# A hybrid two-layer decoder on one core: the stick-breaking rounds in a written order, and the value projections regrouped

## The chip, the cores and the metric

The kernel runs on one core of one Trainium2 chip. The metric is the device time of one execution in microseconds (us), the median of several runs. Names of engines are those of the profile: PE (TensorE, matmuls), PEld (its weight loads), DVE (VectorE), ACT (ScalarE), POOL (GpSimd) and SP (SyncE, which issues DMAs).

## The reference

The reference is a trunk of two decoder layers over 512 positions of width 1024. Each layer has a mixer and a gated feed-forward part with a short causal convolution. The change touches only the mixer of the second layer (`odd_mixer`):

```
cq, ck, cv, sq, sk, sv = split_cols(h @ w_in, ODD_SPLITS)
o_dil = dilated_attention(groups(cq), groups(ck), groups(cv), slopes)
o_sb  = stick_breaking_attention(heads(sq), heads(sk), heads(sv))
return concat([o_dil, o_sb]) @ w_out
```

Dilated attention has three groups of four heads: a plain group (window 128, dilation 1) and two strided groups (dilations 4 and 16). The three are merged by their softmax denominators. Stick-breaking attention has four heads. For each head, with strictly causal entries only:

```
z = (q @ k.T) * scale
log_keep = log_sigmoid(-z)
after = reversed cumsum of log_keep over the keys, without the own key
a = exp(log_sigmoid(z) + after);   o = a @ v
```

## The kernel before, in words

**Numbers.** Every float32 product with weights is made of two rounded parts, a high and a low one (`wh`, `wl`; `xh`, `xl`), by `mm3` (L317 to L319): three matmuls, high by high, high by low, low by high. The class `Weights` loads each weight unit (128 x 1024) into a raw buffer by a DMA on SP's queue (L60), and splits it: ACT casts the high part (L82), DVE subtracts (L83). There are 3 raw buffers (`wraw`) and 5 pairs of split weights (`wh`, `wl`), both used in turn; a load waits until its raw buffer's last split is done, a split waits until the matmuls of the unit five places earlier are done. `W.ahead(n)` puts the splits of all units up to n into the program at that place; `W.depth` is how far ahead `next()` reaches.

**The order of the work.** Outside of `tc.manual_schedule` a scheduler of the compiler decides the order of each engine's instructions. Inside it, the engines that are named keep the order in which the Python code emits. Each engine then works strictly through its own list, and waits where an operand or a buffer isn't ready.

**The stage around the change** (function `odd`), in order:

1. The values of both strided groups (`av`, 512 columns, L1480 to L1495): four tiles of 128 positions, 24 matmuls of 512 columns each. ACT evicts each tile to `vst` (L1493) and issues four DMAs (L1495) which sort its rows by position mod 4 into `cv12`.
2. Four projections of 24 matmuls (`proj_T`, tile `apt`): `sq` and `sk`, each for two pairs of heads.
3. The stick-breaking values (`proj_V(sv)`, tile `apv`, L1458 to L1472): four tiles of 24 matmuls of 256 columns.
4. Two rounds `u` of stick-breaking, each with a pair of heads. Per round: 16 score matmuls (`zp`, L1523), DVE adds the mask (L1527) and takes the minimum with 40 (L1533), ACT takes exp (L1534) and then ln(1 + x) (L1539), DVE takes the maximum with `z` (L1540), and the result is split into `sh` (ACT, L225) and `sl` (DVE, L226). Then, for three blocks of keys from the last to the first, matmuls with a triangle of ones give the sums over later keys (`run` L1552, `cp` L1558), DVE adds them to `z` (L1560, L1562) and ACT takes exp (L1565). At the end 16 matmuls with the values (`osb`, L1571). Between these the code emits the strided groups' eight `proj_T` (list `T12`), four in each round; the scheduler mixes their matmuls with the rounds'. `sh` and `sl` have one buffer each, so the second head's split waits for the first head's sums.
5. Under a written order: four `proj_T` for the plain group, each followed by scores of the strided groups (`score12`, L1606, with exps on ACT, L1617); then the plain group's values (`proj_V(cv)`, again 256 columns), between whose tiles stand the plain group's scores (`score0`, L1631, exps L1640).
6. Still under that order: statistics are exchanged through DRAM (L1661, L1662), `share` turns them into factors, DVE scales (L1679, L1709), PE transposes (L1689, L1719), ACT evicts the transposed blocks to `pt` (L1690, L1720), and PE multiplies them with the values (L1668). `todo` lists eight such blocks, and block n is transposed while block n-1 is multiplied. Here stand also the splits of one output weight `wo` and of the next weight units (`W.ahead`).
7. The output projection (`ao`), then the second feed-forward part.

Of the kernel before, what the change touches and what calls it, by code (L numbers as in the profile page):

```python
# [9 lines left out]
F32 = mybir.dt.float32  # L10
# [7 lines left out]
P = 128  # L18
# [78 lines left out]
def trunk(tc, A, out):  # L97
# [3 lines left out]
    with ExitStack() as top:  # L101
# [1315 lines left out]
        def odd(xnT, pending, order):  # L1417
            xh, xl = xnT
            with ExitStack() as es:
# [4 lines left out]
                cv12 = ap.tile([P, 4, 512], F32, tag="cv12", name="cv12")  # L1424
# [8 lines left out]
                spare = [ap.tile([P, 4, 256], F32, tag=f"spare{n}", name="spare") for n in range(2)]  # L1433
# [4 lines left out]
                sv = sb.tile([P, NT, 256], F32, tag="sv", name="sv")  # L1438
# [4 lines left out]
                def proj_T(dst, scale, permuted, on_act):  # L1443
                    acc = bank("a", "apt")
                    wh, wl = W.next()
                    for k in range(KD):
                        mm3(acc[:], wh[:, k * P:(k + 1) * P], wl[:, k * P:(k + 1) * P],
                            xh[:, k], xl[:, k], k == 0, k == KD - 1)
                    src, d = acc[:], dst[:]
                    if permuted:  # L1450
                        src = src.rearrange("p (t r) -> p r t", r=4)
                        d = d.rearrange("p (r t) -> p r t", r=4)
                    if on_act:
                        ACT.activation(d, src, AF.Copy, scale=scale)
                    else:
                        DVE.tensor_scalar(d, src, scale, None, ALU.mult)

                def proj_V(dst):  # L1458
                    ws = [W.next() for _ in range(2)]

                    def tile_V(i):
                        t = slice(i * P, (i + 1) * P)
                        a = bank("a", "apv")
                        for k in range(KD):
                            wh, wl = ws[k // 4]
                            c = slice((k % 4) * 256, (k % 4 + 1) * 256)
                            mm3(a[:, :256], xh[:, k, t], xl[:, k, t], wh[:, c], wl[:, c], k == 0, k == KD - 1)
                        if i % 2:
                            DVE.tensor_copy(dst[:, i], a[:, :256])
                        else:  # L1470
                            ACT.copy(dst[:, i], a[:, :256])

                    return tile_V
# [3 lines left out]
                ws = [W.next() for _ in range(4)]  # L1477
                W.depth = 5
                for i in ORDER:
                    t = slice(i * P, (i + 1) * P)  # L1480
                    a = bank("a", "av12")
                    at, *parts = pending.pop(0) if pending else (KD, )
                    for k in range(KD):
                        if k == at:
                            for f in parts:
                                f()
                        wh, wl = ws[k // 2]
                        c = slice((k % 2) * 512, (k % 2 + 1) * 512)
                        mm3(a[:], xh[:, k, t], xl[:, k, t], wh[:, c], wl[:, c], k == 0, k == KD - 1)
# [3 lines left out]
                    ACT.copy(st[:], a[:])  # L1493
                    for r in range(4):
                        nc.scalar.dma_start(cv12[32 * i:32 * i + 32, r], st[r::4, :])  # L1495
# [6 lines left out]
                ACT.copy(lead[0:1, 1:2], st[0:1, 0:1])  # L1502
# [6 lines left out]
                tile_V = proj_V(sv)  # L1509
                for i in ORDER:  # L1510
                    tile_V(i)
# [3 lines left out]
                def sb_scores(u):  # L1515

                    zs = [sb.tile([P, 1280], F32, tag="z", name="z", bufs=2) for _ in range(2)]
                    for n, (j0, o0, o1) in enumerate(spans):
                        zp = [bank(t, "zp") for t in ("ss", "nt", "aa")[n]]
                        for j in (j0,) if j0 < 2 else (2, 3):  # L1520
                            for y in range(2):
                                r = slice(y * 64, y * 64 + 64)
                                PE.matmul(zp[y][:, off[j] - o0:off[j + 1] - o0], sk[u][r, j * P:(j + 1) * P],  # L1523
                                          sq[u][r, j * P:], start=True, stop=True)
                        for y in range(2):
                            for j in (j0,) if j0 < 2 else (2, 3):
                                DVE.tensor_tensor(zs[y][:, off[j]:off[j + 1]], zp[y][:, off[j] - o0:off[j + 1] - o0],  # L1527
                                                  smask[:, :S - j * P], ALU.add)

                    sps = []  # L1530
                    for z in zs:
                        sp = sb.tile([P, 1280], F32, tag="sp", name="sp", bufs=2)
                        DVE.tensor_scalar(sp[:], z[:], 40.0, None, ALU.min)  # L1533
                        ACT.activation(sp[:], sp[:], AF.Exp)  # L1534
                        sps.append(sp)
                    return list(zip(zs, sps))

                def sb_softplus(z, sp):
                    ACT.activation(sp[:], sp[:], AF.Ln, bias=1.0)  # L1539
                    DVE.tensor_tensor(sp[:], z[:], sp[:], ALU.max)  # L1540

                def sb_weights(z, sp):
                    sh = sb.tile([P, 1280], F32R, tag="sh", name="sh")
                    sl = sb.tile([P, 1280], F32R, tag="sl", name="sl")
                    split(sh[:], sl[:], sp[:])


                    run = bank("t", "run")
                    for j in reversed(range(NT - 1)):
                        c, n = off[j], S - j * P  # L1550
                        for part in (sh, sl):
                            PE.matmul(run[:, (j + 1) * P:], tri[:, 1], part[:, off[j + 1]:off[j + 2]],  # L1552
                                      start=(j == NT - 2 and part is sh), stop=(part is sl), skip_group_check=True)
                        zp = bank("ssn"[j], "cp")
                        for i in (3, 2) if j == 2 else (j, ):
                            o, w = 256 * (i == 3), S - i * P
                            for part in (sh, sl):
                                PE.matmul(zp[:, o:o + w], tri[:, 0], part[:, off[i]:off[i] + w],  # L1558
                                          start=(part is sh), stop=(part is sl))
                        DVE.tensor_tensor(z[:, c + P:c + n], z[:, c + P:c + n], run[:, (j + 1) * P:], ALU.add)  # L1560
                        w = n + (P if j == 2 else 0)
                        DVE.tensor_tensor(z[:, c:c + w], z[:, c:c + w], zp[:, :w], ALU.add)  # L1562
                        if j < 2:
                            e = slice(c, 1280 if j else off[1])
                            ACT.activation(z[:, e], z[:, e], AF.Exp)  # L1565

                def sb_values(u, a, o):
                    for j in reversed(range(NT)):
                        for n in range(2):
                            h = 2 * u + n  # L1570
                            PE.matmul(o[n * 64:(n + 1) * 64, j * P:], sv[:, j, h * 64:(h + 1) * 64],  # L1571
                                      a[n][:, off[j]:off[j + 1]], start=(j == NT - 1), stop=(j == 0),
                                      skip_group_check=True)

                T12 = [lambda t=t, x=x: proj_T(t[x], (-0.125, 1.0)[t is ck], True, t is cq)
                       for x in range(2, 6) for t in (cq, ck)]
                for u in range(2):
                    zs = sb_scores(u)
                    for _ in range(2):
                        T12.pop(0)()  # L1580
                    for v in zs:
                        sb_softplus(*v)
                    T12.pop(0)()
                    for v in zs:
                        sb_weights(*v)
                    T12.pop(0)()
                    o = bank("o", "osb")
                    sb_values(u, [z for z, _ in zs], o)
                    split(oS[0][:, u], oS[1][:, u], o)


                s12, s0 = {}, {}

# [78 lines left out]
                def turned_to(n):  # L1672
                    tag, pool = (("spare0", ap), ("spare1", ap), ("sl", sb))[n % 3]
                    return pool.tile([P, 4, 256], F32, tag=tag, name="pt")[:]
# [6 lines left out]
                def turn0(i):  # L1681
                    def f():
                        w = span0[i][1]
                        pt = turned_to(i)
# [26 lines left out]
                def turn12(hp, rp):  # L1711
                    def f():
                        s = s12[hp, rp]
                        pt = turned_to(2 * hp + rp).rearrange("p (y a) (b c) -> p y a b c", y=2, b=2)
# [21 lines left out]
                homes = [[(sb, "sq"), (sb, "sk")], [(sb, "sv"), (ap, "tab12")]]  # L1736
# [3 lines left out]
                with tc.manual_schedule(engines={PE.engine, DVE.engine, ACT.engine, POOL.engine}):  # L1740
# [7 lines left out]
                    tile_V = proj_V(cv)  # L1748
# [90 lines left out]
def layout(inputs):  # L1839
# [37 lines left out]
    r["od_w_v"] = np.stack([rows(w[:, 1536:1792], 4), rows(w[:, 2816:], 4)])  # L1877
# [63 lines left out]
```

## Time and profile before

| what | value |
| --- | --- |
| median of 3 runs | 1120.62 us (1119.51 to 1121.82) |
| the profiled execution's own time | 1120.28 us |
| its span in the profile | 1118.2 us |
| mean granted TensorE clock | 0.998 |
| stage 2 (`sq`, `sk`) | from 593.4 us |
| stage 3 (`sv`) | from 615.3 us |
| stage 4, first and second round | from 627.1 and 659.1 us |
| stage 5, projections, then `cv` | from 691.1 and 718.2 us |
| stage 6 | from 734.6 us |

The profile is of one execution. The page gives each engine's busy time, the chain of work that ended last, and the costliest groups of instructions. The trace behind it answers further views: a timeline by engine (start, length, engine, line, operation, tile written and tiles read, and in square brackets the idle time before it and what ended that), busy time by stretches of time, waits, and DMA issues. In the timeline, rows of `SPq`, `ACTq` and `POOL ... DMA` are issues of DMAs. PE's matmuls are pipelined, so that the distance from start to start is their pace, and the length shown is longer.

### The profile page before, as it was taken

The numbers are of one execution on the slowest core, as the hardware profiler recorded it, in microseconds if no ns is written. First come the engines' busy times: TensorE is split into PE (matmuls) and PEld (weight loads), VectorE is DVE, ScalarE is ACT, GpSimd is POOL, SyncE is SP. The second block draws the span as 40 slices with busy tenths as digits, with TensorE's granted clock in tenths as the row PEclk, the third lists the DMA queues.
The fourth block names the chain that finished last, engine by engine and source line by source line (L and its number), as shares of the span: only waits on it lengthen the run. The fifth ranks groups of instructions, "written<-read, shape, count | busy, mean of one in ns | idle before, by whom it ended". The sixth has DMA issues, their size and how long they took to land.

```text
span 1118.2 us, 18152 instructions
## 1 busy us (share of the span) xinstructions
PE 1106.7 (99%) x6792; PEld 960.0 (86%) x6792; DVE 898.4 (80%) x1509; ACT 642.6 (57%) x1091; POOL 126.7 (11%) x241
## 2 busy tenths in 40 slices
PE   9999999999999999999999999999999999999997
PEld 8876677898999999887888877888999999988876
DVE  6667676488999999999874576677899999999896
ACT  5555576346676665556543554565466666656562
POOL 2311143320000000000032111013100000000002
PEclk9999999999999999999999999999999999999999
DMA  8797998458556555354728999847656566545461
GB/s 298 236 248 210 250 273 210 136 177 204 170 174 194 181 184 180 125 180 141 255 91 278 296 293 291 235 118 199 201 157 198 172 188 189 175 127 161 151 207 75
DMA packets 72743, 218.81 MB, mean 196 GB/s; under 512 B 10064, under 2 KB 11216, under 8 KB 64464
## 3 DMA queue, kind: packets, MB, share of 16 engines
q1 hardware_dynamic: 61248, 148.06, 40.0%
q0 software_dynamic: 9920, 67.12, 24.0%
q10 hardware_dynamic: 1488, 2.49, 0.7%
q8 instruction: 53, 0.87, 0.3%
q14 instruction: 34, 0.28, 0.1%
HBM read 210.26 MB, written 73.43 MB: 254 GB/s over the span
## 4 chain that ended last, share of the span: by engine, by line
PE 93%; DVE 2%; ACT 2%; issue 1%; DMA 1%; POOL 0%; SPq 0%; POOLq 0%; DVEq 0%; ACTq 0%
PE u L319 12%; PE u L318 12%; PE u L317 12%; PE acc L317 6%; PE acc L318 6%; PE acc L319 6%; PE apt L317 3%; PE apt L318 3%; PE apt L319 3%; PE ao L317 2%; PE ao L319 2%; PE ao L318 2%; PE aqk L317 1%; PE p L319 1%; PE p L318 1%; PE p L317 1%
## 5 line engine op out<-in xcount | busy, mean ns | idle before, releaser
L83 DVE TENSOR_TENSOR wl<-wraw,wh 128x1024 fp32r<-128x1024 f32 x246 | 298.3, 1218 | 40.4 <-ACT wh L82 39.5
L82 ACT CAST wh<-wraw 128x1024 fp32r<-128x1024 f32 x246 | 254.7, 1047 | 117.2 <-PE u L318 24.2
L319 PE MATMUL u<-xh,wl 128*128 128x256 f32 (+1 forms) x640 | 195.0, 305 | 0.0
L317 PE MATMUL u<-xh,wh 128*128 128x256 f32 (+1 forms) x640 | 195.0, 305 | 0.0
L318 PE MATMUL u<-xl,wh 128*128 128x256 f32 (+1 forms) x640 | 194.8, 304 | 0.0
L319 PEld LDWEIGHTS u<-xh,wl 128*128 128x128 f32 x640 | 122.3, 191 | 5.5 <-DVE wl L83 0.7
L317 PEld LDWEIGHTS u<-xh,wh 128*128 128x128 f32 x640 | 122.3, 191 | 5.0
L318 PEld LDWEIGHTS u<-xl,wh 128*128 128x128 f32 x640 | 122.3, 191 | 5.0
L319 PE MATMUL u<-gh,wl 128*128 128x256 f32 x384 | 108.7, 283 | 0.0
L317 PE MATMUL u<-gh,wh 128*128 128x256 f32 x384 | 108.7, 283 | 0.0
L318 PE MATMUL u<-gl,wh 128*128 128x256 f32 x384 | 108.7, 283 | 0.0
L318 PE MATMUL acc<-wl,gh 128*128 128x512 f32 (+1 forms) x234 | 90.8, 388 | 0.0
L317 PE MATMUL acc<-wh,gh 128*128 128x512 f32 (+1 forms) x234 | 90.5, 389 | 0.3 <-DVE uu L688 0.3
L319 PE MATMUL acc<-wh,gl 128*128 128x512 f32 (+1 forms) x234 | 90.6, 387 | 0.0
L232 POOL TENSOR_TENSOR rv<-ms,epst 128x1 f32<-128x1 f32 x39 | 12.7, 326 | 631.5 <-ACT junk L284 286.9
L481 ACT ACTIVATE y<-u,cw 128x512 f32<-128x512 f32 x88 | 67.8, 777 | 26.2 <-PE u L319 26.2
L318 PEld LDWEIGHTS u<-gl,wh 128*128 128x128 f32 x384 | 73.7, 192 | 0.1
L317 PEld LDWEIGHTS u<-gh,wh 128*128 128x128 f32 x384 | 73.7, 192 | 0.1
L319 PEld LDWEIGHTS u<-gh,wl 128*128 128x128 f32 x384 | 73.7, 192 | 0.0
L162 POOL DMA_DIRECT2D ws<-in_ffn_up_q x72 | 52.3, 728 | 159.0 <-DMA ws<-ws 82.6
L487 DVE SCALAR_TENSOR_TENSOR y<-u,cw,y 128x510 f32<-128x510 f32 x88 | 65.5, 746 | 2.2
L485 DVE SCALAR_TENSOR_TENSOR y<-u,cw,y 128x511 f32<-128x511 f32 x88 | 65.0, 742 | 0.9 <-ACT y L481 0.9
(373 smaller groups left out, 2493.5 us busy)
## 6 DMA issues: line engine op xcount, KB each, us to landing
ws<-in_ffn_up_q POOLq DMA_DIRECT2D x48, 768.0 KB, 12.0
wraw<-ws SPq DMA_DIRECT2D x128, 256.0 KB, 3.1
wraw<-in_ffn_up_q SPq DMA_DIRECT2D x96, 256.0 KB, 2.9
wraw<-in_ffn_w_down SPq DMA_DIRECT2D x44, 512.0 KB, 3.5
ws<-ws POOLq DMA_DIRECT2D x16, 768.0 KB, 14.0
ws<-in_ffn_up_q POOLq DMA_DIRECT2D x24, 512.0 KB, 6.1
wraw<-in_ffn_w_up SPq DMA_DIRECT2D x24, 512.0 KB, 4.5
wraw<-in_od_w_dqk SPq DMA_DIRECT2D x12, 512.0 KB, 10.6
```

The costliest lines, as they stand in the source:

```text
L82: self.nc.scalar.copy(h[:, :w], raw[:, :w])
L83: self.nc.vector.tensor_tensor(l[:, :w], raw[:, :w], h[:, :w].bitcast(F32), ALU.subtract)
L162: nc.gpsimd.dma_start(tiles[j][c][:].rearrange(wide, q=4), src.rearrange(wide, q=4), accum_op=op, max_dma_last_dim=8192)
L232: POOL.tensor_tensor(v[:, :n], ms, epst[:, :n], ALU.add)
L317: PE.matmul(o, lh, rh, start=first, stop=False, skip_group_check=more)
L318: PE.matmul(o, lh, rl, start=False, stop=False, skip_group_check=more)
L319: PE.matmul(o, ll, rh, start=False, stop=last, skip_group_check=more)
L481: ACT.activation(y[:, z], u[z], AF.Identity, bias=c[:, 3:4], scale=c[:, 2:3])
L485: DVE.scalar_tensor_tensor(y[:, z, 1:], u[z][:, :S - 1], c[:, 1:2], y[:, z, 1:], ALU.mult, ALU.add)
L487: DVE.scalar_tensor_tensor(y[:, z, 2:], u[z][:, :S - 2], c[:, 0:1], y[:, z, 2:], ALU.mult, ALU.add)
```

## The change

1. **Values regrouped.** The plain group's values and the stick-breaking values are projected together at stage 1: 4 x 24 matmuls of 512 columns, evicted by ACT in two copies of 256 columns into `cv` and `sv`. The strided groups' values are projected where `cv` was, in stage 5, and there ACT copies each tile to `vst` and issues the four DMAs. The weight units are put in that order.
2. **Projections in parts.** `proj_T` becomes a generator, `T_parts`, which stops after each of the eight k-steps (three matmuls). `fill(n)` emits n k-steps of the strided groups' projections, and after each finished projection calls `W.ahead(W.pos + 4)`.
3. **Rounds in a written order.** Both rounds stand under `manual_schedule` for PE, DVE and ACT. `stick(u)` does every step for both heads one after the other, with `fill` between, and the second head has `sh` and `sl` of its own, in the room of `cv12` and `spare`, which are allocated after the rounds.
4. `turned_to` counts its own calls, and takes halves of one tile `spare`.

```diff
-        units += [(A["od_w_v12"][u], 1024) for u in range(4)]
+        units += [(A["od_w_v"][u], 1024) for u in range(4)]
         units += [(A["od_w_sqk"][u], 1024) for u in range(4)]
-        units += [(A["od_w_v"][1, u], 1024) for u in range(2)]
         units += [(A["od_w_dqk"][u], 1024) for u in range(4, 12)]
         units += [(A["od_w_dqk"][u], 1024) for u in range(4)]
-        units += [(A["od_w_v"][0, u], 1024) for u in range(2)]
+        units += [(A["od_w_v12"][u], 1024) for u in range(4)]
         units += [(A["od_w_out"][k], 1024) for k in range(2, 4)]
...
-                    st = chp.tile([P, 512], F32, tag="s", name="vst")
-                    ACT.copy(st[:], a[:])
-                    for r in range(4):
-                        nc.scalar.dma_start(cv12[32 * i:32 * i + 32, r], st[r::4, :])
+                    ACT.copy(cv[:, i], a[:, :256])
+                    ACT.copy(sv[:, i], a[:, 256:])
...
-                tile_V = proj_V(sv)
-                for i in ORDER:
-                    tile_V(i)
...
+                T12 = [T_parts(t[x], (-0.125, 1.0)[t is ck], True, t is cq) for x in range(2, 6) for t in (cq, ck)]
+                fills = [f for part in T12 for f in [part] * KD]
+
+                def fill(n):
+                    for _ in range(n):
+                        next(fills.pop(0))
+                        if len(fills) % KD == 0:
+                            W.ahead(W.pos + 4)
+
+                def stick(u):
...
+                    for y in range(2):
+                        for n, (j0, o0, o1) in enumerate(spans):
                             for j in (j0,) if j0 < 2 else (2, 3):
+                                DVE.tensor_tensor(zs[y][:, off[j]:off[j + 1]], zp[n][y][:, off[j] - o0:off[j + 1] - o0],
                                                   smask[:, :S - j * P], ALU.add)
+                        DVE.tensor_scalar(sps[y], zs[y][:], 40.0, None, ALU.min)
+                        ACT.activation(sps[y], sps[y], AF.Exp)
+                        fill(4)
+                    for y in range(2):
+                        ACT.activation(sps[y], sps[y], AF.Ln, bias=1.0)
+                    shs = [sb.tile([P, 1280], F32R, tag="sh", name="sh"),
+                           ap.tile([P, 2048], F32R, tag="cv12", name="sh")[:, :1280]]
+                    sls = [sb.tile([P, 1280], F32R, tag="sl", name="sl"),
+                           ap.tile([P, 2048], F32R, tag="spare", name="sl")[:, :1280]]
+                    for y in range(2):
+                        DVE.tensor_tensor(sps[y], zs[y][:], sps[y], ALU.max)
+                        split(shs[y][:], sls[y][:], sps[y])
+                        fill(4)
+                    fill(4)
+
+                    run = [bank(t, "run") for t in "to"]
                     for j in reversed(range(NT - 1)):
...
+                        for y in range(2):
+                            for part in (shs[y], sls[y]):
+                                PE.matmul(run[y][:, (j + 1) * P:], tri[:, 1], part[:, off[j + 1]:off[j + 2]], ...)
+                            cp = bank(("sn", "ns", "ss")[j][y], "cp")
...
+                        for y, z in enumerate(zs):
+                            DVE.tensor_tensor(z[:, c + P:c + n], z[:, c + P:c + n], run[y][:, (j + 1) * P:], ALU.add)
+                            DVE.tensor_tensor(z[:, c:c + w], z[:, c:c + w], cps[y][:, :w], ALU.add)
+                            if j < 2:
+                                e = slice(c, 1280 if j else off[1])
+                                ACT.activation(z[:, e], z[:, e], AF.Exp)
+                        fill(3 if j else 6)
...
+                with tc.manual_schedule(engines={PE.engine, DVE.engine, ACT.engine}):
+                    depth, W.depth = W.depth, 0
+                    left = stick(0)
+                    left()
+                    left = stick(1)
+                    left()
+                    W.depth = depth
...
-                    tile_V = proj_V(cv)
+                    project = proj_V()
+
+                    def tile_V(i):
+                        a = project(i)
+                        st = chp.tile([P, 512], F32, tag="s", name="vst")
+                        ACT.copy(st[:], a)
+                        for r in range(4):
+                            nc.scalar.dma_start(cv12[32 * i:32 * i + 32, r], st[r::4, :])
+
                     tile_V(3)
                     score0(3, "ss")
```

More of the change, by code (lines that the diff above doesn't have):

```diff
@@ L1554, in sb_weights @@
[L1554 to L1560, printed above, removed]
@@ L1561, in sb_weights @@
[L1561 to L1567 removed]
+                        w = n + (P if j == 2 else 0)
+                        cps = []
+                        for y in range(2):
+                            for part in (shs[y], sls[y]):
+                                PE.matmul(run[y][:, (j + 1) * P:], tri[:, 1], part[:, off[j + 1]:off[j + 2]],
+                                          start=(j == NT - 2 and part is shs[y]), stop=(part is sls[y]),
+                                          skip_group_check=True)
+                            cp = bank(("sn", "ns", "ss")[j][y], "cp")
+                            for i in (3, 2) if j == 2 else (j, ):
+                                o, m = 256 * (i == 3), S - i * P
+                                for part in (shs[y], sls[y]):
+                                    PE.matmul(cp[:, o:o + m], tri[:, 0], part[:, off[i]:off[i] + m],
+                                              start=(part is shs[y]), stop=(part is sls[y]))
+                            cps.append(cp)
```

112 lines of the change are left out of this document (41 added, 71 removed).

## The prediction

> **What bounds the kernel now.** I read the page first, then busy time by stretches, then the chain, then the timelines of the stage in `odd`.
>
> ```profile
> span 1118.2 us, 18152 instructions
> ...
> PE 1106.7 (99%) x6792; PEld 960.0 (86%) x6792; DVE 898.4 (80%) x1509; ACT 642.6 (57%) x1091; POOL 126.7 (11%) x241
> ...
> PE 93%; DVE 2%; ACT 2%; issue 1%; DMA 1%; POOL 0%; SPq 0%; POOLq 0%; DVEq 0%; ACTq 0%
> ```
>
> PE is busy all the time and carries 93% of the chain. Only less PE work, or less waiting by PE, makes the kernel faster; every new wait of PE makes it slower by its length. So I ask where PE waits now in this stage (columns: stretch; its length; busy time and count of PE, PEld, DVE, ACT, POOL; granted clock; DMA share; GB/s).
>
> ```profile
> 627.10:659.10 32.00, 31.82 (x158) 24.39 (x158) 24.42 (x34) 20.28 (x21) 5.82 (x8) 1.00 1.03 247
> 659.10:691.10 32.00, 31.84 (x158) 24.43 (x157) 22.98 (x33) 18.16 (x19) 4.78 (x7) 1.00 1.02 283
> ...
> 718.20:734.60 16.40, 16.06 (x130) 14.71 (x131) 10.28 (x61) 10.63 (x42) 0.00 (x0) 1.00 0.34 99
> 734.60:752.50 17.90, 17.90 (x188) 14.09 (x187) 14.19 (x43) 12.67 (x24) 3.37 (x5) 1.00 0.52 149
> ```
>
> In the two rounds PE idles 0.2 us of 32, and after the values not at all. DVE and ACT are busy for 20 to 24 of 32 us: a written order that lets them take turns can make PE wait.
>
> **The change, part by part.** All sums are made against the profiled execution's own time, 1120.28 us (span 1118.2 and 2.1 around it); the median of the runs shown, 1120.62, lies 0.3 higher.
>
> *Values projected as one.* 192 matmuls of 256 columns become 96 of 512. Their pace, from evictions on DVE that are two tiles (48 matmuls) apart:
>
> ```profile
> 604.72 0.69 DVE L1456 TENSOR_SCALAR sk<-apt 128x512 f32<-128x512 f32 x1 [1.01 <-PE apt L319]
> ...
> 615.60 0.69 DVE L1456 TENSOR_SCALAR sk<-apt 128x512 f32<-128x512 f32 x1 [1.75 <-PE apt L319]
> ...
> 618.48 0.42 DVE L1469 COPY sv<-apv 128x256 f32<-128x256 f32 x1 [0.21 <-PE apv L319]
> ...
> 624.24 0.42 DVE L1469 COPY sv<-apv 128x256 f32<-128x256 f32 x1 [5.33 <-PE apv L319]
> ```
>
> At 512 columns 10.88/48 = 0.227 us, so a k-step of three takes 0.68 and a projection 5.45; at 256 columns 5.76/48 = 0.120. 192 x 0.120 - 96 x 0.227 = 1.3; by the whole stage (96 matmuls from 615.3 to 627.1) it is 1.8. I take **-1.5**.
>
> *The written rounds.* A round now lasts from one group of scores to the next, 32.04 us, and in it stands one wait, for DVE's add:
>
> ```profile
> 627.08 2.36 PE zp L1523 x16
> ...
> 648.58 0.34 DVE z L1560
> ...
> 659.12 2.36 PE zp L1523 x16
> ```
>
> Without it the same work takes 31.7. In the new order, after the scores PE has 4 + 4 + 4 + 4 + 4 = 20 k-steps (13.6 us), and then the sums of both heads. What must be done until then is seen in the first round of before:
>
> ```profile
> 635.68 0.58 ACT L1454 ACTIVATE cq<-apt 128x512 f32<-128x512 f32 x1
> 636.16 1.04 ACT L82 CAST wh<-wraw 128x1024 fp32r<-128x1024 f32 x1
> 637.21 1.28 ACT L1539 ACT_TABLE_LOAD   x1
> 638.51 2.44 ACT L1539 ACTIVATE sp<-sp 128x1280 f32<-128x1280 f32 x2
> ```
>
> ```profile
> 641.34 1.27 ACT L225 CAST sh<-sp 128x1280 fp32r<-128x1280 f32 x1 [0.40 <-DVE sp L1540]
> ```
>
> ```profile
> 639.82 2.89 DVE L1540 TENSOR_TENSOR sp<-z,sp 128x1280 f32<-128x1280 f32 x2 [1.36 <-ACT sp L1539]
> ...
> 643.23 1.48 DVE L226 TENSOR_TENSOR sl<-sp,sh 128x1280 fp32r<-128x1280 f32 x1
> ...
> 660.38 3.26 DVE L1527 TENSOR_TENSOR z<-zp,smask 128x512 f32<-128x512 f32 x8
> 663.56 1.55 DVE L1533 TENSOR_SCALAR sp<-z 128x1280 f32<-128x1280 f32 x2
> ```
>
> ```profile
> 645.84 0.22 PE L1552 MATMUL run<-sh,tri 128*128 128x128 f32 x1
> ...
> 646.55 0.38 PE L1552 MATMUL run<-sh,tri 128*128 128x256 f32 x1
> ```
>
> Count from the start of the scores. They end at 2.4, the first projection at 7.9. DVE starts masks at 1.0 to 1.3, ends the second minimum 4.8 later, and the second exp (1.25 after it) ends at 7.1 to 7.4. In ACT's written list the eviction `cq` of the first projection stands next: 8.0 to 8.55; the cast of a weight to 9.55, the table load to 10.85, ln of the first head to 12.1. Now the list of DVE in the built program reads: maximum, `sl`, maximum, `sl`. Each `sl` waits for ACT's `sh`, and the second maximum stands behind the first `sl`. So six steps follow one another: 1.45 + 1.27 + 1.48 for each head, with hand-overs of about 0.1: first `sl` at 16.5, second at 20.8. PE arrives at the first head's sums at 2.4 + 0.1 + 13.6 = 16.1 and needs 0.7 for them (the two `run` rows), so at the second head's low part at 16.9: it waits 0.4 and 3.5, together 4.0. Before, the scheduler put the second head's split beside the first head's sums and put 24 k-steps ahead of them.
>
> Later blocks: 3 k-steps and the other head's sums lie between an add on DVE and the matmul that needs it; the adds (0.29 to 0.69 each) with one weight's subtraction among them end 0.5 us or more before PE comes. A round is 31.7 + 4.0 = 35.7, 3.65 longer: **+7.3** for two. Bounds: with all hand-overs gone and a maximum overlapped 2.6 a round, with late weights on ACT 4.3: 5.2 to 8.6.
>
> [...]
>
> *The strided groups' values moved late.* Four DMAs on ACT's list go with each tile. What they cost there:
>
> ```profile
> 588.48 0.60 ACT L1493 COPY vst<-av 128x512 f32<-128x512 f32 x1
> 589.10 2.41 ACTq L1495 DMA_DIRECT2D cv<-vst  x4
> 591.55 0.59 ACTq L1498 DMA_DIRECT2D trif<-in_sb_tri  x1
> 592.18 1.05 ACT L82 CAST wh<-wraw 128x1024 fp32r<-128x1024 f32 x1 [3.11 <-issue]
> ```
>
> ACT does nothing else while it issues: 2.4 us a tile. In stage 1 nothing waited for that, so leaving it out there gains nothing. In stage 5, PE's tiles now last 5.5 instead of 2.9 us, and the exps of the scores, 2.4 or 4.8 us later on ACT, stay covered; the first scaled block is ready 0.4 us before the last tile ends (call that end E; nothing is lost, but the cover is thin). After E it isn't covered. ACT copies the last tile and issues until E + 3.1, and only then evicts the transposed blocks.
>
> ```profile
> 734.65 1.94 PE t L1689 x16
> 736.59 1.02 PE oT L1668 x16
> ```
>
> ```profile
> 735.12 2.09 ACT L1690 COPY pt<-t 128x512 f32<-128x512 f32 x4
> ```
>
> PE transposes two blocks until E + 1.9 and waits for the first copy (0.55) until E + 3.7: **1.8**. The four DMAs land 4.3 us after issue (the DMA view's row below), by E + 7.4, before their first use at E + 11.
>
> ```profile
> cv<-vst ACTq DMA_DIRECT2D x16, 64.0 KB, 4.3
> ```
>
> Then the weights. Four units, not two, are held until E, so two output weights that were split before E now stand after it, in front of the first feed-forward unit, all three between two evictions. Whose raw buffer that unit gets decides more:
>
> ```profile
> 711.20 6.19 SPq L60 DMA_DIRECT2D wraw<-in_ffn_w_up  x2
> ...
> 743.00 8.07 SPq L60 DMA_DIRECT2D wraw<-in_ffn_w_up  x4
> ```
>
> ```profile
> 741.75 1.23 DVE L83 TENSOR_TENSOR wo<-wraw,wo 128x1024 fp32r<-128x1024 f32 x1
> ```
>
> ```profile
> 748.41 1.04 ACT L82 CAST wh<-wraw 128x1024 fp32r<-128x1024 f32 x1 [0.51 <-DMA wraw<-in_ffn_w_up]
> ```
>
> Before, two such units were loaded early, and only the third began at 743.0, when `wo` had been split (741.75 + 1.23), and was there at 748.4: 5.4 us. Now the first one is the load that waits for `wo`. ACT casts `wo` at E + 7.8, DVE ends it at E + 10.1, the unit lands at E + 15.5. Its cast holds ACT until E + 16.6, and behind it wait the evictions that PE needs at E + 14.5 (blocks of 1.02 and six `ao` matmuls from E + 3.7 on); the first is done at E + 17.1: **2.6**. DVE's subtraction, behind the cast, stands ahead of the last block's scaling: 0.4. Together **+4.8**. Bounds: only the first wait (1.8), and 7 if the two next units, which wait in the same way, and the eviction of the result behind them add 2.
>
> *At nothing:* eviction of `cv` and `sv` by ACT in stage 1 (PE runs on; 0.37 each if it didn't); POOL's list, which is the same and begins about 2 us earlier; the SP list, where `w_v12` stands behind the projections' units; projections begun 11.8 us earlier, whose units are split up to five ahead.
>
> **Sum:** -1.5 + 7.3 + 4.8 = +10.6; 1120.28 + 10.6 = **1130.9 us**.
>
> **The rivals.**
> 1. *The tail is mostly hidden.* If units land sooner, only the 1.8 stays: -1.5 + 7.3 + 1.8 = +7.6, 1127.9. For it: DMA share only 0.52 there. Against: 5.4 us were measured with that share.
> 2. *Faster: the written order feeds PE in time.* It decides at one point: the second head's low part must be there within 9.0 us of the first projection's end (12 k-steps and 0.7). Then each round gains the 0.34 wait and stage 6 loses nothing: -1.5 - 0.7 = 1118.1. Against: the six steps alone take 8.4 us, and eviction, cast, load and ln stand before them.
> 3. *Weights late.* DMA share is 1.02 to 1.03 in the rounds; a unit 2 us late holds ACT ahead of each ln, up to +4: 1135.
> 4. *The clock.* All windows show 1.00. If a stop of PE brought half the clock for the 3.6 us of work behind it in each round, +7.2: 1138. [...] No row here shows a lower clock.
>
> That the change isn't in force is excluded: the built lists stand in the new order.
>
> **How the numbers follow.** Forecast 0.62, hidden tail 0.15, faster 0.08, late weights 0.09, clock 0.03, a cancellation to about no change 0.03. The bounds add to 5.2 (-1.8 + 5.2 + 1.8) and 14.3 (-1.3 + 8.6 + 7), 1125.5 to 1134.6; to take in late weights the range is 1125 to 1136. A measurement of this kernel tells about 0.2% (2.2 us) from no change: faster 0.08, same 0.03, slower 0.89.
>
> **What would show it.** In the changed profile: `run` at the second head's `sl` waits about 3.5 us for DVE L225 (the line moves by one) in both rounds; rounds of 35.7 us; ACT's four issues of 2.4 us behind the last values tile and a PE wait of 1.8 for the first copy; a cast that waits for `in_ffn_w_up` with PE behind it; tiles of 512 columns at 5.45. Wrong it is if PE stays at 99% busy in the rounds, or if DVE's second maximum runs during the first `sh`.

## The result, and the profile after

The changed kernel takes **1140.30 us** (median of 4 executions, 1138.85 to 1142.56) against 1120.39 before: a ratio of 1.0174 with a 95% interval from 1.0161 to 1.0188. It is 1.7% slower. The sign was forecast; the size was not: +19.9 us where +10.6 was predicted, and the range ended at 1136.

The page of the changed kernel:

```profile
span 1139.8 us, 17970 instructions
...
PE 1114.9 (98%) x6696; PEld 963.2 (85%) x6696; DVE 897.5 (79%) x1505; ACT 643.6 (56%) x1095; POOL 125.7 (11%) x241
...
PEclk9999999999999999999999889989999999999999
```

PE is busy 8.2 us longer with 96 matmuls fewer, and the last line points to the reason: in three of the 40 slices PE's granted clock is below nine tenths. Busy time by stages (columns as in the prediction; round one, round two, projections, scores with the late values, and from the last values tile to the last value product):

```profile
615.36:652.84 37.48, 34.14 (x158) 26.54 (x157) 23.35 (x33) 17.87 (x18) 6.34 (x9) 0.91 1.02 256
652.84:690.44 37.60, 34.25 (x159) 26.58 (x157) 23.30 (x35) 19.41 (x20) 5.79 (x9) 0.91 1.02 299
690.44:717.41 26.97, 26.97 (x162) 21.53 (x161) 15.03 (x56) 12.60 (x31) 3.21 (x4) 1.00 1.03 291
717.41:744.16 26.75, 26.41 (x130) 20.89 (x129) 9.72 (x60) 12.03 (x44) 0.00 (x0) 1.00 0.19 60
744.16:773.68 29.52, 22.00 (x190) 17.57 (x188) 16.39 (x44) 14.94 (x25) 3.81 (x6) 0.85 0.63 197
```

Against the stretches of before (32.00, 32.00, 27.10, 16.40, 17.90) that is +5.5, +5.6, -0.1, +10.35 and +11.6. The first scores start 11.7 us earlier (615.36, not 627.08). Together +21.2 of the 21.6 us by which the spans differ.

PE in round one, every row with a wait and the round's ends:

```profile
615.36 2.43 PE L1525 MATMUL zp<-sq,sk 64*128 64x512 f32 x16
...
631.45 0.22 PE L1554 MATMUL run<-sh,tri 128*128 128x128 f32 x1
632.01 0.33 PE L1554 MATMUL run<-sl,tri 128*128 128x128 f32 x1 [0.34 <-DVE sl L225]
...
634.70 0.39 PE L1554 MATMUL run<-sh,tri 128*128 128x128 f32 x1 [1.85 <-ACT sh L224]
636.23 0.47 PE L1554 MATMUL run<-sl,tri 128*128 128x128 f32 x1 [1.14 <-DVE sl L225]
...
652.84 2.43 PE L1525 MATMUL zp<-sq,sk 64*128 64x512 f32 x16
```

The stop is where it was forecast, 0.34 + 1.85 + 1.14 = 3.3 us (forecast 4.0). DVE shows the turns:

```profile
627.64 1.49 DVE L1542 TENSOR_TENSOR sp<-z,sp 128x1280 f32<-128x1280 f32 x1 [1.36 <-ACT sp L1536]
630.46 1.49 DVE L225 TENSOR_TENSOR sl<-sp,sh 128x1280 fp32r<-128x1280 f32 x1 [1.33 <-ACT sh L224]
631.87 1.48 DVE L1542 TENSOR_TENSOR sp<-z,sp 128x1280 f32<-128x1280 f32 x1
634.68 1.49 DVE L225 TENSOR_TENSOR sl<-sp,sh 128x1280 fp32r<-128x1280 f32 x1 [1.32 <-ACT sh L224]
```

Twice it waits 1.3 us for ACT's cast. The second maximum needs nothing but ln, which has ended at 628.77 (ACT's row: 626.33, 2.44 long); DVE is free at 629.13, and the maximum starts 2.7 us after that.

What was not in the sum is seen when the same stretch is cut every 3.41 us (after the length: PE's busy time and matmuls; third from the end, the granted clock). Round one:

```profile
631.41:634.82 3.41, 1.21 (x8) 0.76 (x6) 2.09 (x3) 1.43 (x2) 0.79 (x1) 1.00 1.00 252
634.82:638.23 3.41, 2.27 (x8) 1.97 (x9) 3.31 (x5) 2.06 (x2) 0.80 (x1) 0.50 1.03 221
638.23:641.65 3.42, 3.42 (x10) 2.66 (x9) 1.28 (x3) 0.00 (x0) 0.44 (x1) 0.50 1.03 216
641.65:645.06 3.41, 3.41 (x20) 3.04 (x19) 1.86 (x4) 1.90 (x3) 0.38 (x1) 1.00 1.05 259
```

and behind the last values tile:

```profile
744.05:747.46 3.41, 2.02 (x18) 1.69 (x16) 3.38 (x16) 0.61 (x2) 0.00 (x0) 1.00 0.12 43
...
757.70:761.11 3.41, 1.26 (x6) 0.69 (x4) 0.27 (x1) 0.93 (x1) 1.25 (x2) 1.00 1.02 321
761.11:764.53 3.42, 2.77 (x18) 2.24 (x19) 3.28 (x6) 3.09 (x6) 0.00 (x0) 0.50 1.00 237
764.53:767.94 3.41, 3.41 (x24) 2.76 (x22) 0.14 (x1) 0.00 (x0) 0.53 (x1) 0.50 0.99 275
767.94:771.35 3.41, 0.69 (x4) 0.30 (x2) 1.12 (x1) 2.19 (x4) 0.00 (x0) 1.00 0.90 364
771.35:774.77 3.42, 3.42 (x19) 2.56 (x19) 1.15 (x3) 0.90 (x2) 0.00 (x0) 0.50 0.53 172
```

In this trace the clock is exactly 1.00 or 0.50 in each cut and changes only at its edges; all its eight changes between 600 and 800 us lie on one grid of 3.413 us (from 634.82 to 774.77 are 41 steps). After the cuts with PE busy 0.69 to 1.26 us the next was halved; after 2.02 it was not; and the halved clock came back only after cuts in which PE was busy throughout, not after 2.27 or 2.77. In a round two cuts are halved, and round one is 5.5 us longer: PE idles 3.3 us of it (37.48 less 34.14), against 0.2 before, and is busy 2.3 us longer with the same 158 matmuls.

The other traces agree. Cut by their own grids, all fifteen had half clock after every cut with PE busy 1.69 us or less and after none with 1.93 or more; between these, one cut of 1.82 (e11) was followed by half clock and six of 1.70 to 1.91 were not. The full clock came back after cuts with 3.35 us or more, never after 2.90 or less.

The kernel before shows it too, at its very end, where PE runs out of work:

```profile
1110.65:1114.06 3.41, 0.70 (x6) 0.50 (x5) 2.75 (x9) 0.51 (x2) 1.04 (x3) 1.00 0.40 156
1114.06:1117.47 3.41, 0.00 (x0) 0.00 (x0) 0.71 (x2) 0.00 (x0) 0.00 (x0) 0.50 0.41 154
```

It costs nothing there (PE is busy 0.00 us in the halved cut), but half clock from 1114.06 to the end of the span at 1118.2 is why the mean clock of before is 0.998 and not 1.

PE's waits from 585 to 800 us (in all, times, longest): two lines for the rounds, three for the stretch behind the last values tile:

```profile
PE run L1554 <- ACT sh L224: 3.7, 2, 1.9
PE run L1554 <- DVE sl L225: 3.0, 4, 1.2
PE oT L1668 <- ACT pt L1725: 2.8, 1, 2.8
PE ao L316 <- ACT og L224: 2.7, 1, 2.7
PE oT L1668 <- ACT spare L1695: 2.0, 1, 2.0
```

ACT's rows for the three waits:

```profile
744.98 2.42 ACTq L1760 DMA_DIRECT2D cv<-vst  x4
747.43 2.06 ACT L1695 COPY spare<-t 128x512 f32<-128x512 f32 x4 [2.49 <-issue]
...
760.18 1.04 ACT L82 CAST wh<-wraw 128x1024 fp32r<-128x1024 f32 x1 [3.65 <-DMA wraw<-in_ffn_w_up]
...
769.16 1.04 ACT L82 CAST wh<-wraw 128x1024 fp32r<-128x1024 f32 x1 [4.96 <-DMA wraw<-in_ffn_w_up]
```

PE's rows of the same work at full and at half clock (16 value products, 8 transposes):

```profile
750.17 1.09 PE L1668 MATMUL oT<-spare,cv 128*64 128x128 f32 x16
...
756.47 1.09 PE L1724 MATMUL t<-ident,s 128*128 128x128 f32 x8
...
761.76 2.45 PE L1668 MATMUL oT<-pt,cv 128*64 128x128 f32 x16 [2.80 <-ACT pt L1725]
764.14 1.97 PE L1724 MATMUL t<-ident,s 128*128 128x128 f32 x8
766.04 1.98 PE L1668 MATMUL oT<-spare,cv 128*64 128x128 f32 x16
...
771.40 2.28 PE L1668 MATMUL oT<-spare,cv 128*64 128x128 f32 x16
```

Of the waits, the first is ACT's issuing, the other two are casts that wait for a feed-forward unit with PE's next copy queued behind them. SP issues the first of these loads at 754.61, 0.03 us after DVE ends the split of `wo` (from 753.35, 1.23 long), and it lands after 5.5 us. The second, issued at 756.87, lands after 5.3, in time for its cast. The cast at 769.16 is that of the third, issued at 758.00:

```profile
wraw<-in_ffn_w_up SPq DMA_DIRECT2D x1, 512.0 KB, 11.1
```

### The profile page after: what moved, and what is told of

It is laid out like the page before. It is cut to its first block, busy times and chain, and to the rows that moved or that the text cites. A ratio compares the mean times of both kernels' runs of the same rounds, so it can differ in the third digit from the quotient of the medians.

```text
span 1139.8 us, 17970 instructions
## 1 busy us (share of the span) xinstructions
PE 1114.9 (98%) x6696; PEld 963.2 (85%) x6696; DVE 897.5 (79%) x1505; ACT 643.6 (56%) x1095; POOL 125.7 (11%) x241
## 4 chain that ended last, share of the span: by engine, by line
PE 84%; DVE 7%; DMA 3%; ACT 3%; issue 2%; POOL 0%; ACTq 0%; POOLq 0%; DVEq 0%
PE u L318 12%; PE u L316 12%; PE u L317 12%; PE acc L316 4%; PE acc L317 4%; PE acc L318 4%; PE apt L316 2%; PE apt L317 2%; PE apt L318 2%; PE ao L316 2%; PE ao L318 2%; PE ao L317 2%; DVE wl L83 2%; PE p L318 1%; PE p L317 1%
## 5 line engine op out<-in xcount | busy, mean ns | idle before, releaser
L231 POOL TENSOR_TENSOR rv<-ms,epst 128x1 f32<-128x1 f32 x39 | 11.6, 296 | 647.5 <-ACT junk L283 296.8
## 6 DMA issues: line engine op xcount, KB each, us to landing
ws<-ws POOLq DMA_DIRECT2D x16, 768.0 KB, 13.6
```

The costliest lines, as they stand in the source:

```text
L231: POOL.tensor_tensor(v[:, :n], ms, epst[:, :n], ALU.add)
```

## The experiments

All are edits of the changed kernel unless it says otherwise. The table gives the median, the ratio to the kernel before run beside it (95% interval), both rounds, the stretch from the last values tile to the last value product, and the time at half clock between 600 and 800 us (the last three from the profiled execution, by its timeline).

| version | us | ratio | rounds | behind the last tile | half clock |
|---|---|---|---|---|---|
| changed kernel | 1140.30 | 1.0174 (1.0161-1.0188) | 37.5, 37.6 | 29.5 | 23.9 |
| e1 maxima first | 1135.06 | 1.0120 (1.0105-1.0135) | 32.2, 32.3 | 31.6 | 10.2 |
| e2 PE kept busy | 1141.29 | 1.0172 (1.0156-1.0187) | 35.0, 35.1 | 29.6 | 13.7 |
| e3 weights early | 1132.64 | 1.0111 (1.0090-1.0132) | 36.6, 36.7 | 20.2 | 6.8 |
| e4 values by SP | 1140.03 | 1.0169 (1.0149-1.0190) | 37.4, 37.5 | 24.2 | 17.1 |
| e12 = e3 + e4 | 1131.11 | 1.0083 (1.0068-1.0098) | 37.8, 37.8 | 18.0 | 13.7 |
| e13 = e12 + e2 | 1127.66 | 1.0053 (1.0038-1.0068) | 35.0, 35.1 | 18.4 | 0 |
| e5 rounds of before | 1134.76 | 1.0100 (1.0066-1.0133) | 32.0, 32.1 | 31.5 | 10.2 |
| e8 = e5 + e3 + e4 | 1120.83 | 0.9984 (0.9965-1.0003) | 32.0, 32.1 | 17.9 | 0 |
| e7 = e1 + e3 | 1126.19 | 1.0030 (1.0011-1.0050) | 32.2, 32.3 | 26.8 | 6.8 |
| e10 = e1 + e4 | 1129.42 | 1.0069 (1.0051-1.0088) | 32.2, 32.3 | 22.8 | 3.4 |
| e6 all three | 1119.46 | 0.9980 (0.9959-1.0001) | 31.1, 31.5 | 18.0 | 0 |
| e14 = e6, one split sooner | 1119.07 | 0.9982 (0.9969-0.9995) | 31.0, 31.4 | 17.9 | 0 |

**Is it the taking of turns? (e1)**

```
                         DVE.tensor_tensor(sps[y], zs[y][:], sps[y], ALU.max)
+                    for y in range(2):
                         split(shs[y][:], sls[y][:], sps[y])
                         fill(4)
```

> DVE's list takes both heads' maxima before the first subtraction, so that the second maximum runs beside the first cast. Theory (taking turns makes the stop): the second low part is there 2.7 us earlier; PE's stop in each round falls from 3.3 to about 0.9 us, the granted clock stays at 1.00 there, and a round lasts 32.6 instead of 37.5 us: 1130.5 us. If the stop alone counts and the clock costs nothing: 1135.4. Rival (eviction, weight cast, table load and ln ahead of both heads set the stop, the order of DVE does not): within 1 us of the changed kernel, 1139 to 1141.

In the rounds the theory holds: 32.2 and 32.3 us, no wait above 0.5, no halved clock. That is 10.6 us gained there, but the ratio fell by 0.0054 only, 6 us. In the profiled executions the span fell by 7.5: the rounds began 0.9 us later, and the stretch behind the last values tile took 2.1 us more (31.6 against 29.5). This stage came 10 us earlier, into the DMA traffic of the sums (POOL's transfers of `ws`, which add up feed-forward weights in DRAM), which ends near 720 us in both traces:

```profile
PE oT L1669 <- ACT spare L1726: 5.6, 1, 5.6
PE t L1695 <- DVE s L1685: 2.6, 1, 2.6
```

ACT's four issues for the second late tile took 6.04 us there:

```profile
720.84 0.47 ACTq L1761 DMA_DIRECT2D cv<-vst  x1
723.12 0.47 ACTq L1761 DMA_DIRECT2D cv<-vst  x1
723.73 0.51 ACTq L1761 DMA_DIRECT2D cv<-vst  x1
726.40 0.47 ACTq L1761 DMA_DIRECT2D cv<-vst  x1
```

In the changed kernel the same four, 10 us later, took 2.48. An issue itself is as short in e1 (0.47 to 0.51); ACT stood still between them. The last three issues each began 0.03 to 0.07 us after an earlier DMA had landed: the load of an output weight (issued at 706.96, 16.1 us to landing) and the two DMAs of the first exchange (711.00, 12.7 us; 723.73, 2.6 us). The first tile's four issues, at 714.11 in the full traffic (DMA share 1.03), took 2.47. As I read it, the traffic reached ACT through DMAs that landed late, not by making an issue longer. After that the exps came late, then the shares, then the scaling that PE waited 2.6 us for. I had not expected this.

**Has the halved clock a price of its own? (e2, e13)** Twelve matmuls, overwritten afterwards, fill the gap between the two heads:

```
                         for y in range(2):
+                            for _ in range(12 * (j == 2 and y == 1)):
+                                PE.matmul(run[1], tri[:, 0], xh[:, 0], start=True, stop=True, skip_group_check=True)
```

> In each round 12 further matmuls of 512 columns (2.7 us of PE, their result is overwritten) stand where PE now waits for the second head, so the waiting work starts no earlier, but PE isn't idle. Theory (the halved clock is a cost of its own, brought by the idle time): the granted clock stays at 1.00 in the rounds, the second head's low part comes at the same time, and a round lasts 35.0 instead of 37.5 us: 1135.4 us. Rival (the slow matmuls behind the stop come from something else, DMA traffic or the operands): clock and round as in the changed kernel, 1140 us. A second rival (the added matmuls cost their own time): 1145 us.

The rounds did as the theory said: 35.0 and 35.1 us, 2.5 less with *more* work for PE, at full clock. But the ratio did not move, and the 1135.4 us of the theory was missed. In the profiled execution, the quickest of four, the span is 3.1 us shorter; where the others lost the gain no trace shows. I repeated it where the stage behind was mended (e12, below):

> The kernel with the mended tail, and in each round 12 further matmuls of 512 columns (overwritten) where PE would wait for the second head. With nothing behind the rounds that gives time back, the median shows the price of the halved clock. Theory: rounds of 35.05 us at a clock of 1.00, 3 to 5 us less than the kernel with the mended tail in all: 1124.7 us. Rival (the halved clock costs nothing in the end): the same as the mended tail within 1 us.

Round one of e12, then of e13 (the second rounds: 37.77 and 35.12):

```profile
615.80:653.55 37.75, 34.35 (x157) 26.79 (x156) 23.40 (x33) 17.88 (x18) 6.92 (x10) 0.91 1.02 258
```

```profile
615.74:650.73 34.99, 34.06 (x169) 26.62 (x168) 23.13 (x33) 17.87 (x18) 6.34 (x9) 1.00 1.03 258
```

With 12 matmuls more a round is 2.7 us shorter, at a clock of 1.00 instead of 0.91. The second head's low part is taken up at the same time, 20.9 us after the first scores, in both; the gain lies behind it. Here the median falls too, by 3.5 us (the rounds give 5.4 of the spans; later stages give 1.6 back, for which I have no cause). The DMA share is nearly the same in both (1.02 and 1.03), so the traffic isn't what slows the matmuls. Shown: the halved clock costs time of its own, about 2.7 us a round.

**Late weights (e3), ACT's issuing (e4), both (e12).** The edits:

```
                     score0(3, "ss")
+                    wo2.append(W2.next())
+                    W.ahead(W.pos + 1)
...
-                        if n == 3:
-                            wo2.append(W2.next())
```

```
-                            nc.scalar.dma_start(cv12[32 * i:32 * i + 32, r], st[r::4, :])
+                            nc.sync.dma_start(cv12[32 * i:32 * i + 32, r], st[r::4, :])
```

> Two output weights are split before the last three values tiles instead of behind them, so that two raw buffers come free and the first two feed-forward units are loaded some 20 us before they are cast. Theory (a raw buffer held until the last values tile makes the units late, their casts hold ACT, and PE waits): the two PE waits of 2.8 and 2.7 us and the two stretches of half clock behind them go, the wait of 2.0 for the first copy stays: 1130.7 us. If the casts were held by something else (the free pair of wh and wl, DVE's subtractions): 1137 to 1141.

> The sixteen DMAs that spread the strided groups' values are issued by SP instead of ACT. Theory (ACT's issuing of 2.4 us holds the first copy of transposed blocks): PE's wait of 2.0 us goes and what ACT does behind it comes 2.4 us earlier: 1138 us. Rival (the wait is hidden by the later waits for feed-forward units, whose loads hang on another chain): 1140 us, with the two later waits longer by 2 us in all.

> The changed kernel with both edits of the tail (two output weights split early, DMAs issued by SP), the written rounds untouched. Theory: rounds of 36.6 to 37.5 us with their stop and one or two stretches of 3.4 us at half clock each, 18 us from the last values tile to the last value product: 1120.6 - 1.7 + 10 + 0.3 = 1129.2 us. If the tail still waits: 1132 to 1136.

With early weights the stretch falls from 29.5 to 20.2 us and both waits go; that it is only the wait for the first copy that remains is shown by e12, where SP issues as well: 18.0, as before the change. By SP alone (e4) nothing is gained that the interval could show. Its trace has no wait for the first copy, but 3.2 and 1.1 us for the weights, so the later waits did not grow as the rival said, and the stretch is 5.3 us shorter (24.2), with two halved cuts less. Against that, the first scores start 2.6 us later in this trace (617.96); over all traces but e11's they start between 614.98 and 617.96. Why the median shows nothing of the 5.3 us stays open. The rounds of e3 last 36.6 where those of e12 last 37.8: one halved cut in each against two, with the same waits of 1.9 and 1.2. Where the stop falls on the grid is what differs: by PE's pace (matmuls of 512 columns 0.43 us apart, not 0.23) and the grid the halving began at about 636.4 in round one of e3, when the stop had just ended (636.32), and at about 635.9 in that of e12, 0.8 us before its end (636.67), so that e12's first halved cut was not busy throughout (about 2.6 us) and the next was halved too.

**What is left without the written rounds (e5, e8).** The functions and the loop of the rounds are those of before, the values stay as changed; e8 adds the edits of e3 and e4.

> The rounds of the kernel before stand in the changed kernel; the merged projection and the late values stay. Theory (each written round costs 5.4 us, 3.0 net of waiting and 2.45 of halved clock, and the rest of the change 10 us behind the last values tile): rounds of 32.05 us, the last values tile ends at 734 instead of 744 us, and the stretch from there to the last value product stays at 29.5 us: 1129.5 us. Rival (what comes behind the rounds is longer when it comes 10 us earlier, beside the DMA traffic of the sums, as with the maxima taken first): that stretch lasts 31 to 32 us or the tiles longer: 1131.5 to 1135 us.

> The rounds of the kernel before, with both edits of the tail (two output weights split early, DMAs issued by SP). Theory: rounds of 32.05 us, no wait behind the last values tile: 1119.3 us, 0.7 above the version with mended written rounds, and 1 below the kernel before. Rival (the sums' traffic holds this stage): 1122 to 1125 us.

e5 went as its rival said: the rounds are back at 32.0, and the stretch behind grows to 31.5, as in e1 (the first exchange takes from 711.58 to 723.84). So what each part costs can't simply be added up: the stretch behind the last tile costs 13.6 us over the 17.9 of before when it comes early (e5), and 11.6 in the changed kernel. In the ratios (e5 takes 0.74% off, e12 0.91%, both together, e8, 1.90%) the difference lies within the intervals. With both edits of the stretch, the early arrival costs nothing (17.9).

**The corners (e7, e10).** Maxima first, with one of the two edits each.

> Both maxima first and two output weights split early; ACT still issues the DMAs of the strided values. Theory (DMAs that ACT issues while the sums' traffic runs take it 6.0 instead of 2.4 us, the first scaling comes 2.6 us late, and the first copy waits 2.0): rounds of 32.2 us, 20.2 + 2.6 us from the last values tile to the last value product: 1124 to 1125 us. Rival (the late scaling came from the late weights): 1121.5 to 1122.5 us.

> Both maxima first and the strided values' DMAs issued by SP; the weights stay late. With the maxima alone, and with maxima and early weights, this is the third corner of a square. Theory (the traffic of the sums reaches PE through ACT's issuing, which took 6.0 us there, and late weights are a cost of their own): rounds of 32.2 us, no late scaling ahead of the first transposes, and 24 to 25 us from the last values tile to the last value product, as when SP issued with the old rounds (24.2): 1125 to 1126 us. Rival (late weights behave worse when the stage comes 10 us earlier, whoever issues): 31 us there, 1132 us.

e7's median is 1 to 2 us above the theory. Its trace is of the slowest of ten executions (1129.55): ACT's four issues at 721.58 took 2.44 us and not 6.0, no scaling came late, but the third unit landed 8.0 us after its issue and PE waited 4.2. e10's trace agrees with the theory (22.8 us), but it is the quickest of eight executions, 1124.1; the others took 1128.9 to 1134.5 at a mean clock of 0.993 to 0.994, against 0.997, and no trace shows where. The median, 1129.42, lies 3 us above the theory. What those executions did stays open.

**One part alone, on the kernel before (e11).** The two projections merged ahead of the rounds, strided values left early, nothing between the late scores.

> The kernel before with one part of the change alone: plain group and stick-breaking values projected as one, ahead of the rounds; the strided values stay early and nothing stands between the plain group's scores. Theory (a merged projection saves 1.7 us of PE, and what is moved late is cover for the exps and the exchange): PE waits 8 to 10 us between the last scores and the first transposes, the clock halves once there, and the kernel is slower than before: 1126 to 1131 us. Rival (the exps and scalings are short enough): 1119 us.

1138.98 us, ratio 1.0153 (1.0136 to 1.0170), 8 us above the theory. PE waits for the scalings as forecast, if less long:

```profile
PE t L1688 <- DVE s L1678: 5.9, 1, 5.9
PE apt L316 <- DVE z L1526: 3.9, 1, 3.9
PE run L1551 <- DVE z L1559: 2.1, 3, 1.4
```

But the scheduler also put the rounds in another order, with waits of 3.9 and 2.1 that no edit was meant to make. The run shows that the late tiles are cover; it gives no price.

**All three (e6), and one split sooner (e14).** e6 has the edits of e3 and e4, both maxima first, and the first projection's eviction and the weight cast behind the casts of both high parts:

```
-                        fill(4)
+                        fill(4 - y)
...
-                        split(shs[y][:], sls[y][:], sps[y])
-                        fill(4)
-                    fill(4)
+                    for y in range(2):
+                        split(shs[y][:], sls[y][:], sps[y])
+                    fill(13)
```

> Three edits together: both maxima first and the eviction and weight cast behind both casts of the high parts, two output weights split early, the DMAs of the strided values issued by SP. Theory (these are all the places where the time went): rounds of 31.7 us without a wait or a halved clock, and no wait of PE behind the last values tile: 1120.4 - 1.7 - 0.7 + 0.6 (a wait of 1.0 in the scores, 0.3 before) = 1118.6 us. Rival (the traffic of the sums, which ends near 720 us, holds the stage that now comes 10 us earlier): 1121 to 1125 us, with a wait for values or for the exchanged sums.

```profile
617.34:648.39 31.05, 31.05 (x158) 24.32 (x157) 22.59 (x33) 17.78 (x18) 5.78 (x7) 1.00 1.02 259
733.55:751.56 18.01, 18.01 (x190) 14.39 (x188) 11.68 (x33) 12.74 (x23) 3.68 (x5) 1.00 0.58 168
```

The same 158 matmuls as in the round of 37.48 us now take 31.05. The interval of the ratio still touches 1. e14 changes one condition in the loop over the transposed blocks (`if n > 3:` becomes `if n > 2:`):

> The kernel with all three edits, and the split of the second early output weight one step sooner behind the last values tile, so that the third feed-forward unit is loaded about 2 us sooner. In the kernel with all three edits its cast still held ACT for 1.2 us, and two of ten executions took 1123.4 and 1125.0 us at a lower clock. Theory (these executions had the unit late, a stop of PE and a halved clock): no execution above 1122 us, the median 0.2 to 0.8 us lower than with the three edits, 2 to 3 us below the kernel before in the same runs. Rival (the spread comes from elsewhere, since the kernel before shows it too): one or two executions above 1123 us again, ratio to the kernel before 0.998.

1119.07 against 1120.76 in the same runs: 0.18% faster, interval 0.9969 to 0.9995. It is the only version whose interval excludes 1, and by little; the ratio of e6 is the same. One of its eleven executions took 1123.08 us, as the rival said. But the edit did not bring the third unit in time: the load was issued 2.5 us sooner than in e6 (741.63, 744.18) and took 5.6 instead of 3.7 us, and its cast waits 1.80 us where it waited 1.18. So whether the late unit makes the spread is not tested, and its cause stays open.

## Why the prediction was wrong

- **Values merged, -1.5:** right. First scores 11.72 us earlier, the late stage 10.35 longer: -1.4.
- **The stop in the rounds, 4.0:** right in place and cause, 3.3 measured. e1 shows that DVE's list makes it. The wait of 0.34 us that I took off the rounds of before was DVE's add, as the chain lists it; PE's own row at 648.97 has 0.18.
- **The first wait behind the last tile, 1.8, and the second, 2.6:** right, 2.0 and 2.8. e12 and e3 show both causes.
- **The two next units, put in the bounds at up to 2:** too small. The second was in time. The third was issued as soon as the split before it was done, but it needed 11.1 us to land, at a DMA share of 1.01, where I counted 5.4 for a unit; its cast held ACT 5 us and PE 2.7. The 5.4 was one load of before; its later loads of the same kind, issued at 748.47 and 750.75, took 9.6 and 8.9.
- **The clock, rival 4:** the step that failed. I put it at nothing in the sum and gave it a chance of 0.03 because no row of before that I had read shows a lower clock, and looked for it in the rounds alone. But before has no stop of PE in these stages to show it with, and my windows ended at 780 us; the one at 1110.65 shows it. In the rounds PE is busy 2.3 and 2.4 us longer, and e13 against e12 gives 2.7 us a round (the rival's 3.6 was an estimate that no run shows). Behind the last tile two more stretches were halved: the value products of 16 matmuls, 1.09 us at full clock, took 2.45, 1.98 and 2.28, and 8 transposes 1.97 for 1.09, 4.3 us together. That part is read from the trace, not isolated.

The halving did not take one unbroken gap here: with 1.21 and 1.26 us of work in a cut of 3.41 the next was halved, and in the rounds a matmul with the high part (634.70) stands in the middle of the stop. I had thought that such a matmul would save the clock.

By the sums: forecast -1.5 + 7.3 + 4.8; measured -1.4 + 11.1 (6.4 more of waiting, 4.7 of longer PE work) + 11.6 (7.5 of waiting, 4.1 of longer PE work). Of the 10.7 us that were missing, the longer PE work, which I put down to the clock, is 8.8, and the third unit 2.7; the stop in the rounds was 0.9 smaller than forecast.

## What to carry to other kernels

Where PE is the bound, price a new wait of PE twice: its length, and the halved clock that may stand behind it. In these traces it did when the waits in one cut of 3.41 us added up, broken or not, to 1.72 us or more, and did not when they added up to 1.48 or less (3.41 less 1.69, and less 1.93). Loads that waited for buffers released late came close behind one another here, and the third took 11.1 us where the first two took 5.5 and 5.3: follow the chain until a load is early again. And a stage that comes earlier can meet DMA traffic that it used to miss: e1 gained 10.6 us in the rounds and 6 in the whole.

## What the runs showed of the hardware

- Filling the stop of PE with useless matmuls paid here: 12 more in a round made it 2.7 us shorter, at a clock of 1.00 instead of 0.91 (e13 against e12).
- Issuing four DMAs of 64 KB from ACT took 2.4 to 2.5 us, with the DMA engines nearly idle (share 0.15 at 744.98) or full (1.03 at 714.11 in e1); ACT did nothing else meanwhile (busy 0.00 us from 744.98 to 747.40). The 6.04 us of e1 are four issues of 0.5 us and the time between them, in which earlier DMAs landed.
- Executions of one kernel differ by up to 10 us (e10: 1124.1 to 1134.5, mean clocks of 0.997 to 0.993). The kernel before does it too, more rarely: of the 26 executions beside e5 to e8 the median is 1121.52, and three took 1126.0 to 1127.6, at clocks of 0.995 and 0.996. No trace of such an execution was taken.
